# A two-block transformer step on one core: first rope angles on GpSimd, modulation columns by products with ones, lower parts of the first half on VectorE

## The chip, the cores and the metric

The kernel runs on one core of a Trainium2 chip, as one launch. The metric is the device time of the launch in microseconds (us), as the median of several runs.

## The reference, cut to what matters

Two blocks follow each other on one sequence of 1024 tokens of width 1024, all in float32. The first has two layers (differential attention with 8 heads, then latent attention with 8 heads), the second a layer of three mixers and a feed-forward part. Each layer begins in the same way:

```python
mod = silu(c) @ ada_w + ada_b                  # [1024] @ [1024, 3*1024]
shift, scale, gate = split(mod, 3)
h = rmsnorm(x, norm_g) * (1 + scale) + shift
proj = h @ w_in                                # q, k, v, z of all heads
q, k = rope(q, positions), rope(k, positions)  # cos and sin of positions * inv
...
x = x + gate * (o @ w_out)
```

So a layer's first projection needs `scale` and `shift`, each a sum over 1024 rows of a 1024 x 1024 block of `ada_w`, and the first scores need the cosines and sines of the positions.

## The kernel before, in words

Tokens lie along the free dimension: `h` is 8 chunks of 128 channels by two halves of 512 tokens. Every float32 operand of a large product is split into a rounded upper part ("hi") and a lower part ("lo", the rest), and a product of two operands is three products (`mm3`, line 192). The engines' instruction orders are made by a scheduler from the order in which the program is written, from priorities (`ahead`) and from costs that it assumes; each engine then works through its own list in order. All loads and stores are issued from SyncE (SP), also in order, with up to eight outstanding.

The start of layer 0 (`layer0`, line 899 on) is this:

- `load_x` loads x as 8 tiles of 128 tokens; `turn_x` squares and sums them on ScalarE, makes the reciprocal root mean (`rr`), and transposes the tiles on TensorE into `xt0` and `xt1`, one for each half of the tokens.
- `modulation_first` (lines 337 to 360) makes `scale0`, then `shift0`. Eight tiles of `ada_w` (128 rows of the sum each, 512 KB) are loaded into `h4` buffers. Tiles 0 to 3 are scaled by their element of silu(c) and added up on VectorE (lines 347 and 349) in `acc`; tiles 4 to 7 go through TensorE as products with a column of `cs` (line 352) into a row of 1024 sums in PSUM. `sum_cols` (lines 327 to 334) adds `acc` up over its 128 partitions: eight 128 x 128 transposes into two PSUM tiles and two VectorE reductions (line 334). The row in PSUM is copied by ScalarE (line 356) and turned into a column by eight one-row products with a one (line 359); line 360 adds the two.
- `rope_tables` (lines 250 to 279) loads the positions (line 261), makes the angles modulo 2 pi by eight instructions on VectorE (lines 265 to 273) and takes their absolute value, cosine and sine on ScalarE (lines 275 to 277), with a change of the activation table before and after (lines 276 and 279).
- `make_h` (lines 414 to 437) makes h = xt * acol * rr + shift in hi and lo. For half 0 the product is already there (`scaled`, line 915). Even chunks: ScalarE rounds hi (line 433) and VectorE makes lo (line 434). Odd chunks: ScalarE writes the sum (line 429) and rounds it (line 430), and GpSimd subtracts (line 169).
- `qk_rope` loads the first head's q and k weights (line 628), casts hi on ScalarE (line 632), makes lo on GpSimd (line 169), projects both halves (line 192: 96 products of 128 x 128 by 128 x 512 for the first head), turns them with the tables (lines 610 to 614) and moves the pieces into place by DMA (line 676, `move`). The scores (lines 681 and 682) read what was moved.

Later modulations (`modulation`, lines 297 to 325) have all eight tiles on VectorE (lines 316 and 318) and end in `sum_cols` as well: four in layer 0 during the heads (`late`), six for the second block during the heads of layer 1. Their tiles in layer 0 take `wr` buffers, of which there are two, shared with the weights.

## Time and profile before

| | |
|---|---|
| runs | 2959.03, 2968.55, 2955.31 us; median 2959.03 |
| profiled execution | 2964.13 us, its span 2962.4 us |
| TensorE products | 2646.8 us busy, 89% of the span |
| VectorE | 2118.1 us, 71% |
| ScalarE | 1437.1 us, 49% |
| GpSimd | 1291.4 us, 44% |
| mean granted TensorE clock | 0.951 |

Busy time of TensorE is modelled: products overlap, so 89% is not 89% of its peak. Times in the rows below are counted from the start of the span. A row of the timeline names the start, the duration, engine, line, operation and tiles, the number of instructions merged into it, and in brackets how long the engine had been idle and what ended the idling; DVE is VectorE, ACT ScalarE, POOL GpSimd, PE TensorE's products, PEld its weight loads, SPq the queue of SyncE.

### The profile page before, as it was taken

To read this page: it belongs to the slowest core of one execution; us is meant where nothing else is said; L and a number is where in the kernel's file an instruction comes from. 1 tells how busy PE (TensorE), PEld (TensorE's weight loads), DVE (VectorE), ACT (ScalarE), POOL (GpSimd) and SP (SyncE) were. 2 spreads that over 40 slices of the span, in tenths; PEclk is the share of its full clock that TensorE was granted. 3 is DMA by queue.
4 is the path that set the end of the run, shared out by engine and by line. 5 is a ranking of instruction groups with operands and counts; after the bars stand their busy time and mean duration, and the time that the engine had idled before them with its cause. 6 is when DMAs were issued, how large, how long until landed. Compare 5 with 4: busy or idle time off the path is not lost. (4 is left out here: it accounts for less than half of the span.)

```text
span 2962.4 us, 34674 instructions
## 1 busy us (share of the span) xinstructions
PE 2646.8 (89%) x12023; PEld 2136.0 (72%) x12023; DVE 2118.1 (71%) x2888; ACT 1437.1 (49%) x2609; POOL 1291.4 (44%) x775
## 2 busy tenths in 40 slices
PE   7889999899889989999987798887887999997897
PEld 4677777777777767787876587776776777775776
DVE  7687677766653377777677665578868888889874
ACT  5455455555543445454554454467544444444432
POOL 3233333333253352122234332244547887778760
PEclk8899999999999999999998899999998999998998
DMA  7534323233351263333333237424441222234564
GB/s 270 142 90 114 92 66 110 75 79 100 106 172 58 66 226 120 114 104 103 109 126 94 74 93 104 101 64 126 130 152 42 80 79 78 82 105 161 189 237 143
DMA packets 316850, 338.91 MB, mean 114 GB/s; under 512 B 37684, under 2 KB 240516, under 8 KB 316676
## 3 DMA queue, kind: packets, MB, share of 16 engines
q1 hardware_dynamic: 316676, 336.70, 38.6%
q8 instruction: 96, 1.57, 0.2%
q14 instruction: 78, 0.64, 0.1%
HBM read 231.17 MB, written 60.89 MB: 99 GB/s over the span
## 5 line engine op out<-in xcount | busy, mean ns | idle before, releaser
L192 PE MATMUL m<-h,wh 128*128 128x512 f32 x4744 | 1398.8, 404 | 62.3 <-ACT wh L183 16.2
L192 PEld LDWEIGHTS m<-h,wh 128*128 128x128 f32 x4744 | 910.4, 194 | 270.9 <-ACT wh L183 18.8
L192 PE MATMUL m<-h,wl 128*128 128x512 f32 x1472 | 589.8, 402 | 8.8 <-POOL wl L169 8.8
L169 POOL TENSOR_TENSOR wl<-wr,wh 128x1024 fp32r<-128x1024 f32 (+1 forms) x146 | 330.5, 2270 | 479.0 <-ACT wh L183 183.7
L761 ACT CAST pt<-m 128x256 fp32r<-128x256 f32 (+1 forms) x632 | 222.3, 370 | 289.9 <-PE m L757 158.3
L192 PEld LDWEIGHTS m<-h,wl 128*128 128x128 f32 x1472 | 286.9, 195 | 73.9 <-POOL wl L169 11.2
L169 DVE TENSOR_TENSOR pt<-m,pt 128x256 fp32r<-128x256 f32 (+2 forms) x652 | 256.3, 416 | 83.1 <-ACT pt L761 70.8
L741 ACT ACTIVATE e<-s,cf 128x1024 f32<-128x1024 f32 x192 | 214.9, 1121 | 155.1 <-DVE cf L738 139.1
L737 DVE TENSOR_REDUCE cf<-s 128x1 f32<-128x1024 f32 x192 | 232.4, 1217 | 75.8 <-PE s L682 40.5
L757 PE MATMUL m<-cr,e 128*128 128x128 f32 x1240 | 195.4, 282 | 32.9 <-DVE cf L738 14.3
L865 POOL TENSOR_SCALAR e<-e,cf 128x1024 f32<-128x1024 f32 x64 | 82.0, 1281 | 307.8 <-DVE cf L742 278.1
L192 PE MATMUL s<-h,wh 128*128 128x512 f32 x720 | 183.3, 400 | 36.4 <-DVE h L169 17.1
L681 PE MATMUL s<-kk,qq 128*128 128x512 f32 (+3 forms) x376 | 152.5, 411 | 52.6 <-ACT e L741 24.9
L757 PEld LDWEIGHTS m<-cr,e 128*128 128x128 f32 x1240 | 152.6, 145 | 61.5 <-issue 22.3
L1533 DVE SCALAR_TENSOR_TENSOR e<-z,cf,e 128x1023 f32<-128x1023 f32 (+1 forms) x88 | 175.8, 2008 | 24.8 <-ACT e L1531 24.6
L192 PE MATMUL m<-pt,v 128*128 128x512 f32 x768 | 188.7, 395 | 1.0 <-DVE pt L169 0.5
L192 PEld LDWEIGHTS s<-h,wh 128*128 128x128 f32 x720 | 136.9, 192 | 72.7 <-DVE h L169 18.6
L183 ACT CAST wh<-wr 128x1024 fp32r<-128x1024 f32 (+2 forms) x134 | 122.1, 915 | 110.6 <-PE m L192 47.2
L192 PEld LDWEIGHTS m<-pt,v 128*128 128x128 f32 x768 | 144.4, 190 | 32.3 <-DVE pt L169 1.6
L1105 POOL TENSOR_SCALAR e<-e,cf 128x1024 f32<-128x1024 f32 x64 | 73.7, 1154 | 186.6 <-DVE cf L742 182.7
L682 PE MATMUL s<-kk,qq 128*128 128x512 f32 (+3 forms) x376 | 144.4, 392 | 1.5 <-DMA qq<-pt 1.5
L169 DVE TENSOR_TENSOR wh<-wl,wh 128x512 fp32r<-128x512 f32 x90 | 121.7, 1370 | 19.4 <-ACT wh L443 19.2
(368 smaller groups left out, 4549.2 us busy)
## 6 DMA issues: line engine op xcount, KB each, us to landing
wr<-in_w_out_dram SPq DMA_DIRECT2D x48, 512.0 KB
tb<-in_w_ada_dram SPq DMA_DIRECT2D x48, 512.0 KB
wr<-in_w_up_dram SPq DMA_DIRECT2D x47, 512.0 KB
wr<-in_w_in_dram SPq DMA_DIRECT2D x45, 512.0 KB
qq<-ab SPq DMA_DIRECT2D x144, 128.0 KB
wr<-in_ada_w_dram SPq DMA_DIRECT2D x32, 512.0 KB
tf<-act SPq DMA_DIRECT2D x30, 512.0 KB
wr<-in_w_down_dram SPq DMA_DIRECT2D x30, 512.0 KB
```

Source lines behind the costliest of these rows:

```text
L169: (eng or self.nc.vector).tensor_sub(lo, src, hi.bitcast(F32))
L183: nc.scalar.copy(hi, raw)
L192: self.nc.tensor.matmul(out, l, r, start=start and n == 0, stop=stop and n == last)
L681: nc.tensor.matmul(ps, q(0, j), kk[:, ks], start=True, stop=False)
L682: nc.tensor.matmul(ps, q(1, j), kk[:, ks], start=False, stop=stop)
L737: nc.vector.reduce_max(nm, ps, axis=AX, negate=True)
L741: nc.scalar.activation(e, ps, AF.Exp, bias=nm, scale=scale, accum_out=sm)
L757: nc.tensor.transpose(ps[:, i], p[:, kt * 128:(kt + 1) * 128], self.ident)
L761: nc.scalar.copy(hi, ps[:, i:i + m])
L865: nc.gpsimd.tensor_scalar(e1, e1, r1, self.neglam, ALU.mult, ALU.mult)
L1105: nc.gpsimd.tensor_scalar(e, e, r, 1.0, ALU.mult, ALU.mult)
L1533: nc.vector.scalar_tensor_tensor(t[:, sh:], u[:, 0:S - sh], col(i), t[:, sh:], ALU.mult, ALU.add)
```

## The change

1. The first angles are made on GpSimd (`rope_angles(..., nc.gpsimd)`), and are written ahead of the loads of x; cosine and sine (`rope_sin`) stay where they were written. Multiplying by 1/(2 pi) and adding the magic number become one instruction, for both calls; on GpSimd each of the three scaled subtractions is two instructions.
2. `sum_cols` makes eight products of a 128 x 128 block of `acc` with a column of ones instead of eight transposes and two reductions, and its result is read in place by the addition of the bias. All later modulations use it.
3. In `modulation_first` VectorE takes five tiles and TensorE three; the sum on VectorE is added over its partitions by two products with the column of ones into the same PSUM row, and the row is turned by `sum_cols(row, 1)`.
4. In half 0 all eight chunks of h are made like the even ones: hi on ScalarE, lo on VectorE.
5. `load_x` and `turn_x` are called for each half; the tile that only takes the squares is a `tf` in place of a `z`.

```diff
     def rope_tables(self, nme):
+        self.rope_sin(self.rope_angles(nme, self.nc.vector))
+
+    def rope_angles(self, nme, eng):
...
-        nc.vector.tensor_copy(ang, pi)
-        nc.vector.tensor_scalar_mul(ang, ang, inv[:, 0:1])
+        eng.tensor_copy(ang, pi)
+        eng.tensor_scalar_mul(ang, ang, inv[:, 0:1])
         k = pi.bitcast(F32)
-        nc.vector.tensor_scalar_mul(k, ang, 1.0 / two_pi)
-        nc.vector.tensor_scalar_add(k, k, magic)
-        nc.vector.tensor_scalar_sub(k, k, magic)
+        eng.tensor_scalar(k, ang, 1.0 / two_pi, magic, ALU.mult, ALU.add)
+        eng.tensor_scalar_sub(k, k, magic)
         for cc in (c1, c2, c3):
-            nc.vector.scalar_tensor_tensor(ang, k, -cc, ang, ALU.mult, ALU.add)
-        nc.vector.tensor_scalar(ang, ang, lim, -lim, ALU.min, ALU.max)
+            if eng is nc.vector:
+                eng.scalar_tensor_tensor(ang, k, -cc, ang, ALU.mult, ALU.add)
+            else:
+                t = self.t("e", [128, S])
+                eng.tensor_scalar_mul(t, k, -cc)
+                eng.tensor_add(ang, ang, t)
+        eng.tensor_scalar(ang, ang, lim, -lim, ALU.min, ALU.max)
+        return ang, k
+
+    def rope_sin(self, angles):
...
-            self.sum_cols(acc, out)
-            nc.vector.tensor_add(out, out, bcol[:, g * 8:(g + 1) * 8])
+            nc.vector.tensor_add(out, self.sum_cols(acc), bcol[:, g * 8:(g + 1) * 8])
...
-    def sum_cols(self, acc, out):
-        for c0 in range(0, 8, 4):
-            ps = self.pm((128, 4, 128))
-            for j in range(4):
-                nc.tensor.transpose(ps[:, j], acc[:, (c0 + j) * 128:(c0 + j + 1) * 128], self.ident)
-            nc.vector.reduce_sum(out[:, c0:c0 + 4], ps, axis=AX)
+    def sum_cols(self, acc, n=128):
+        cols = self.pm((128, 8))
+        for j in range(8):
+            nc.tensor.matmul(
+                cols[:, j:j + 1], acc[0:n, j * 128:(j + 1) * 128], self.ones1[0:n], start=True, stop=True)
+        return cols
...
-            elif k < 4:
+                continue
+            if k < 5:
                 nc.vector.scalar_tensor_tensor(acc, wt, cs[:, k:k + 1], acc, ALU.mult, ALU.add)
-            else:
-                for i in range(0, 1024, 512):
-                    nc.tensor.matmul(ps[:, i:i + 512], cs[:, k:k + 1], wt[:, i:i + 512], start=k == 4, stop=k == 7)
-        self.sum_cols(acc, out)
-        nc.vector.tensor_add(out, out, bcol[:, g * 8:(g + 1) * 8])
+                continue
+            for i in range(0, 1024, 512):
+                nc.tensor.matmul(ps[:, i:i + 512], cs[:, k:k + 1], wt[:, i:i + 512], start=k == 5, stop=k == 7)
+                if k == 6:
+                    nc.tensor.matmul(ps[:, i:i + 512], self.ones1, acc[:, i:i + 512], start=False, stop=False)
         row = self.t("t2", [128, 1024])
         nc.scalar.copy(row[0:1], ps)
-        cols = self.pm((128, 8))
-        for j in range(8):
-            nc.tensor.matmul(cols[:, j:j + 1], row[0:1, j * 128:(j + 1) * 128], self.ones1[0:1], start=True, stop=True)
-        nc.vector.tensor_add(out, cols, out)
+        nc.vector.tensor_add(out, self.sum_cols(row, 1), bcol[:, g * 8:(g + 1) * 8])
...
-            if c % 2:
+            if c % 2 and scaled is None:
...
+        angles = self.rope_angles("positions", nc.gpsimd)
+        ss = self.small(8, "ss")
+        toks = [self.load_x(half) for half in range(2)]
+        (tiles0, xt0, rr0), (tiles1, xt1, rr1) = [self.turn_x(toks[half], half, ss) for half in range(2)]
...
-        self.rope_tables("positions")
+        self.rope_sin(angles)
```

The change also moves instructions in the lists. ScalarE, from the row copy of `scale0` (into `t_53`) to the first parts of h; `wh` are the cast weights of the first head, `tb` the tables. Before:

```order
L356 COPY t_53_460<-s_418 1x1024
L632 CAST wh_637<-wr_639 128x1024
L632 CAST wh_644<-wr_646 128x1024
L356 COPY t_71_528<-s_486 1x1024
L433 ACTIVATE h_77_559<-z_473,cf 128x512
...
L183 CAST wh_846<-wr_848 128x1024
L891 ACTIVATE cf<-cf 128x1 x2
L433 ACTIVATE h_95_619<-tf_617,cf 128x512
L276 ACT_TABLE_LOAD
L276 ACTIVATE tb_553<-e_540,cf 128x1024
L277 ACTIVATE tb_554<-e_543 128x1024
L279 ACT_TABLE_LOAD
```

In the changed kernel, from the row copy of `scale0` (into `t_57`):

```order
L369 COPY t_57_467<-s_437 1x1024
L288 ACTIVATE e_262<-e_265 128x1024
L638 CAST wh_615<-wr_617 128x1024
L289 ACT_TABLE_LOAD
L289 ACTIVATE tb_535<-e_262,cf 128x1024
L290 ACTIVATE tb_536<-e_265 128x1024
L292 ACT_TABLE_LOAD
L638 CAST wh_622<-wr_624 128x1024
L369 COPY t_73_523<-s_493 1x1024
L443 ACTIVATE h_77_541<-z_480,cf 128x512
L443 ACTIVATE h_78_544<-z_480,cf 128x512
```

The absolute value, the tables and both changes of table now stand ahead of the row copy of `shift0` (`t_73`; `t_71` before), with the first cast of the weights among them.

VectorE, from the end of half 1's products with `rr` to the first lower parts. Before:

```order
L424 SCALAR_TENSOR_TENSOR tf_607<-pt_350,cf,t_31_358 128x512 x2
L334 TENSOR_REDUCE cf<-m_515 128x4
L334 TENSOR_REDUCE cf<-m_521 128x4
L265 CAST e_543<-e_540 128x1024
L354 TENSOR_TENSOR cf<-cf 128x8
L266 TENSOR_SCALAR e_543<-e_543,cf 128x1024
L268 TENSOR_SCALAR e_540<-e_543 128x1024
L269 TENSOR_SCALAR e_540<-e_540 128x1024
L360 TENSOR_TENSOR cf<-m_530,cf 128x8
L270 TENSOR_SCALAR e_540<-e_540 128x1024
L272 SCALAR_TENSOR_TENSOR e_543<-e_540,e_543 128x1024
L434 SCALAR_TENSOR_TENSOR h_77_559<-z_473,cf,h_77_559 128x512
```

In the changed kernel:

```order
L434 SCALAR_TENSOR_TENSOR tf_585<-pt_369,cf,t_37_377 128x512 x2
L370 TENSOR_TENSOR cf<-m_525,cf 128x8
L444 SCALAR_TENSOR_TENSOR h_77_541<-z_480,cf,h_77_541 128x512
L444 SCALAR_TENSOR_TENSOR h_78_544<-z_480,cf,h_78_544 128x512
L444 SCALAR_TENSOR_TENSOR h_79_547<-z_481,cf,h_79_547 128x512
L444 SCALAR_TENSOR_TENSOR h_80_550<-z_481,cf,h_80_550 128x512
```

The addition that ends `shift0` has nothing of the angles or reductions around it.

VectorE, where the lower parts of the first head's second half of q and k (`ab`) stand beside the modulation tile of `gate0` (`t_137`). Before:

```order
L318 SCALAR_TENSOR_TENSOR t_137_888<-wr_1017,cf,t_137_888 128x1024
L169 TENSOR_TENSOR ab_784<-tf_786,ab_784 128x512
L169 TENSOR_TENSOR v_853<-m_881,v_852 128x512
L169 TENSOR_TENSOR ab_785<-tf_786,ab_785 128x512
L318 SCALAR_TENSOR_TENSOR t_137_888<-wr_1116,cf,t_137_888 128x1024
```

In the changed kernel:

```order
L169 TENSOR_TENSOR ab_762<-tf_764,ab_762 128x512
L169 TENSOR_TENSOR v_831<-m_859,v_830 128x512
L169 TENSOR_TENSOR ab_763<-tf_764,ab_763 128x512
L331 SCALAR_TENSOR_TENSOR t_137_866<-wr_995,cf,t_137_866 128x1024
L743 TENSOR_REDUCE cf<-s_914 128x1
```

A modulation tile that stood ahead of the lower parts stands behind them.

## Rows read from the trace of the kernel before

**Rows 1.** Busy time by stage: the stretch, its length, then busy us and instructions of each engine, the mean granted TensorE clock, the busy share of the DMA engines, GB/s.

```profile
20.00:30.00 10.00, 8.20 (x39) 3.62 (x36) 7.04 (x12) 1.78 (x5) 0.00 (x0) 1.00 1.03 410
...
53.00:86.00 33.00, 28.48 (x99) 20.34 (x99) 27.02 (x31) 23.51 (x36) 17.55 (x11) 0.82 0.27 79
...
99.00:115.00 16.00, 6.43 (x18) 4.45 (x19) 10.70 (x15) 4.53 (x9) 1.19 (x1) 0.61 0.82 219
...
120.00:800.00 680.00, 624.09 (x2876) 502.80 (x2875) 501.37 (x882) 372.34 (x714) 212.28 (x115) 0.96 0.33 91
...
1180.00:1480.00 300.00, 292.38 (x1507) 240.70 (x1506) 208.06 (x433) 153.74 (x360) 71.71 (x66) 1.00 0.36 106
```

**Rows 2.** Timeline of the first 60 us, TensorE: the eight one-row products that turn the row of `shift0` (16 records), and the first product with h.

```profile
47.41 1.94 PE L359 MATMUL m<-cf,t 1*128 1x1 f32 x16 [1.15 <-ACT t L356]
...
53.29 1.22 PE L192 MATMUL m<-h,wh 128*128 128x512 f32 x2 [3.94 <-ACT h L433]
```

**Rows 3.** Timeline of ScalarE: casts of the first weights, the row copy of `shift0`, the first part of h, and the tables.

```profile
40.90 1.04 ACT L632 CAST wh<-wr 128x1024 fp32r<-128x1024 f32 x1 [7.91 <-DMA wr<-in_w_in_dram]
...
42.31 1.04 ACT L632 CAST wh<-wr 128x1024 fp32r<-128x1024 f32 x1 [0.36 <-DMA wr<-in_w_in_dram]
...
46.36 1.00 ACT L356 COPY t<-s 1x1024 f32<-1x1024 f32 x1 [3.00 <-PE s L352]
...
52.51 0.72 ACT L433 ACTIVATE h<-z,cf 128x512 fp32r<-128x512 f32 x1 [5.15 <-DVE cf L360]
...
64.73 1.06 ACT L275 ACTIVATE e<-e 128x1024 f32<-128x1024 f32 x1
...
73.47 1.28 ACT L276 ACT_TABLE_LOAD   x1
...
74.77 1.15 ACT L276 ACTIVATE tb<-e,cf 128x1024 f32<-128x1024 f32 x1
...
75.83 1.04 ACT L277 ACTIVATE tb<-e 128x1024 f32<-128x1024 f32 x1
...
76.89 1.28 ACT L279 ACT_TABLE_LOAD   x1
```

**Rows 4.** Timeline of VectorE: half 1's products with `rr`, the start of the angles, the additions of `shift0`, lower parts of h, the last chunk's product, the first turn by the tables, a modulation tile.

```profile
41.27 4.06 DVE L424 SCALAR_TENSOR_TENSOR tf<-pt,cf,t 128x512 f32<-128x512 f32 x6
...
46.45 1.62 DVE L265 CAST e<-e 128x1024 f32<-128x1024 int32 x1
...
47.99 2.29 DVE L354 TENSOR_TENSOR cf<-cf 128x8 f32<-128x8 f32 x1
...
52.32 0.16 DVE L360 TENSOR_TENSOR cf<-m,cf 128x8 f32<-128x8 f32 x1
...
54.31 0.74 DVE L434 SCALAR_TENSOR_TENSOR h<-z,cf,h 128x512 fp32r<-128x512 f32 x1
...
64.63 1.65 DVE L434 SCALAR_TENSOR_TENSOR h<-tf,cf,h 128x512 fp32r<-128x512 f32 x1
...
71.95 0.74 DVE L424 SCALAR_TENSOR_TENSOR tf<-pt,cf,t 128x512 f32<-128x512 f32 x1
...
77.70 0.68 DVE L610 TENSOR_TENSOR tf<-m,tb 128x512 f32<-128x512 f32 x1
...
96.23 1.28 DVE L318 SCALAR_TENSOR_TENSOR t<-wr,cf,t 128x1024 f32<-128x1024 f32 x1 [8.38 <-DMA wr<-in_ada_w_dram]
```

**Rows 5.** Timeline of GpSimd: lower parts of the first weights, of h, a sum of 128 x 1024, a scaling of 128 x 1024.

```profile
42.03 8.23 POOL L169 TENSOR_TENSOR wl<-wr,wh 128x1024 fp32r<-128x1024 f32 x2 [39.88 <-ACT wh L632]
...
63.99 4.69 POOL L169 TENSOR_TENSOR h<-tf,h 128x512 fp32r<-128x512 f32 x3
...
80.86 2.38 POOL L614 TENSOR_TENSOR tf<-tf,tf 128x1024 f32<-128x1024 f32 x1
...
111.84 1.19 POOL L865 TENSOR_SCALAR e<-e,cf 128x1024 f32<-128x1024 f32 x1 [19.30 <-DVE cf L742]
```

**Rows 6.** Timeline of TensorE in the first head: 38 products from the first of these rows to the second; a wait; eight products from 81.97 to 85.30; the last of the projections; the first full scores.

```profile
68.05 0.39 PE L192 MATMUL m<-h,wl 128*128 128x512 f32 x1
...
76.73 0.39 PE L192 MATMUL m<-h,wh 128*128 128x512 f32 x1
...
77.85 0.50 PE L192 MATMUL m<-h,wh 128*128 128x512 f32 x1 [0.73 <-DVE h L434]
...
79.61 0.50 PE L192 MATMUL m<-h,wh 128*128 128x512 f32 x1 [1.03 <-ACT h L430]
...
81.97 0.97 PE L192 MATMUL m<-h,wh 128*128 128x512 f32 x2
...
85.30 0.47 PE L192 MATMUL m<-h,wl 128*128 128x512 f32 x1
...
103.71 0.77 PE L681 MATMUL s<-kk,qq 128*128 128x512 f32 x1 [0.95 <-DMA kk<-ab]
```

**Rows 7.** Groups of the first 150 us by line, engine, operation and shape: count, busy us and mean ns, idle us before.

```profile
L349 DVE SCALAR_TENSOR_TENSOR ab<-h,cf,ab 128x1024 f32<-128x1024 f32 x6 | 7.7, 1280 | 0.1
...
L268 DVE TENSOR_SCALAR e<-e 128x1024 f32<-128x1024 f32 x1 | 0.7, 693 | 0.0
```

**Rows 8.** Timeline at 1188 us, in layer 1: the transposes and reductions of one `sum_cols`.

```profile
1188.58 1.03 PE L333 MATMUL m<-cr,z 128*128 128x128 f32 x8
...
1189.22 0.69 DVE L334 TENSOR_REDUCE cf<-m 128x4 f32<-128x512 f32 x1
```

More of the change, by code (lines that the diff above doesn't have):

```diff
@@ L264, in rope_tables @@
         ang = self.t("e", [128, S])
-        nc.vector.tensor_copy(ang, pi)
-        nc.vector.tensor_scalar_mul(ang, ang, inv[:, 0:1])
+        eng.tensor_copy(ang, pi)
+        eng.tensor_scalar_mul(ang, ang, inv[:, 0:1])
         k = pi.bitcast(F32)
-        nc.vector.tensor_scalar_mul(k, ang, 1.0 / two_pi)
-        nc.vector.tensor_scalar_add(k, k, magic)
-        nc.vector.tensor_scalar_sub(k, k, magic)
+        eng.tensor_scalar(k, ang, 1.0 / two_pi, magic, ALU.mult, ALU.add)
+        eng.tensor_scalar_sub(k, k, magic)
         for cc in (c1, c2, c3):
-            nc.vector.scalar_tensor_tensor(ang, k, -cc, ang, ALU.mult, ALU.add)
-        nc.vector.tensor_scalar(ang, ang, lim, -lim, ALU.min, ALU.max)
+            if eng is nc.vector:
[7 more added lines that the diff above has]
+    def rope_sin(self, angles):
+        nc = self.nc
+        ang, k = angles
         cos, sin = self.t("tb", [128, S]), self.t("tb", [128, S])
@@ L557, in start_pairs, with load_x @@
             drain(g)
-    def load_x(self):
+    def load_x(self, half):
         nc, a = self.nc, self.a
         toks = []
-        for i in range(8):
-            tk = self.t(("kk", "qq")[i // 4], [128, 1024])
+        for i in range(4 * half, 4 * half + 4):
+            tk = self.t(("kk", "qq")[half], [128, 1024])
             nc.sync.dma_start(tk, a["x"][0, i * 128:(i + 1) * 128, :])
@@ L568, in load_x, with turn_x @@
         return toks
[L570 removed]
+    def turn_x(self, toks, half, ss):
         nc = self.nc
[L573 to L595 removed]
@@ new lines, in turn_x @@
+        junk = self.t("tf", [128, 1024])
+        tiles, xt = self.new_xt(("pt",) * 4)
+        hs = slice(4 * half, 4 * half + 4)
+        for i in range(4):
+            nc.scalar.activation(junk, toks[i], AF.Square, accum_out=ss[:, 4 * half + i:4 * half + i + 1])
+        self.rsqrt_mean(ss[:, hs], ss[:, hs], D)
+        t2 = self.t("t2", [128, 2, 512])
+        dg, rr = t2[:, 0].rearrange("p (a b) -> p a b", a=4), t2[:, 1]
+        ps = self.pS((128, 4, 128))
+        for i in range(4):
+            nc.vector.tensor_scalar_mul(dg[:, i], self.ident, ss[:, 4 * half + i:4 * half + i + 1])
+            nc.tensor.matmul(ps[:, i], self.ones_r.bitcast(F32), dg[:, i], start=True, stop=True)
@@ L598, in proj @@
+        nc.vector.tensor_copy(rr, ps.rearrange("p a b -> p (a b)"))
+        for c in range(8):
+            ps = self.pm((128, 4, 128))
+            for i in range(4):
+                nc.tensor.transpose(ps[:, i], toks[i][:, c * 128:(c + 1) * 128], self.ident)
+            (nc.vector.tensor_copy if c % 2 else nc.scalar.copy)(xt[c], ps.rearrange("p a b -> p (a b)"))
+        return tiles, xt, rr
     def proj(self, ws, hts, half, rows=128):
```

25 lines of the change are left out of this document (removed).

## The prediction, made before the changed kernel was run

> **What bounds the kernel now.** I read the stretches first, then the timeline of each engine over the first 105 us, then the groups by line and one later modulation.
>
> The stretches [rows 1] show two regimes. From 120 us on TensorE is busy 624 of 680 us, and in layer 1, from 1180 to 1480, 292 of 300 at a granted clock of 1.00: whatever adds TensorE work there adds time. The start is different. From 53 to 86 us TensorE makes the first head's 96 products and little else at a mean clock of 0.82, and from 99 to 115 it is busy 6.4 of 16 us. The 96 products need 0.228 us each at the full clock (38 products from 68.05 to 76.73, [rows 6]), so 21.9 us. They run from 53.29 [rows 2] to 85.77 [rows 6], 32.5 us. So 10.6 us go to gaps and to the low clock: eight products from 81.97 on start 0.416 us apart [rows 6], the level of 1.2 GHz, after gaps at 77.85, 79.61 and shortly behind.
>
> Who is waited for? h waits for `shift0`: its row is copied at 46.36 [rows 3], turned by 49.35 [rows 2], but added only at 52.32, because VectorE sits on the cast of the angles, on a tiny addition of 2.29 us, and on three more instructions of the angles [rows 4]. Then the lower parts come slowly: 1.65 us each beside GpSimd, 0.74 us without it [rows 4]. The late gaps wait for the last chunk of half 1, whose product with `rr` ran at 71.95 only [rows 4]. The first turn by the tables starts at 77.70 [rows 4], since the sine ended at 76.87 [rows 3]. And the lower parts of half 1's q and k stand behind a modulation tile that kept VectorE idle for 8.38 us until 96.23 [rows 4]. Full scores begin at 103.71, waiting for these moves [rows 6].
>
> **The start, part by part.** The positions go from behind the 16 modulation tiles to the head of SP's queue, past x and all tiles. Their 512 KB take 1.3 us at the 410 GB/s of rows 1, so x and the modulation tiles land about that much later. What stands behind both (the first head's weights) keeps its place in bytes, so its first cast stays at 40.90, where it waited for its data [rows 3]. The later tiles are covered by that, as the list below shows; without this cover they would cost 1.3 us.
>
> VectorE loses eight instructions of the angles, four reductions and two additions, and gains two tile additions of 1.28 us [rows 7] and four lower parts of 0.74 us [rows 4]. The two tile additions fall in the stretch in which it waits for tiles anyway. TensorE loses 16 transposes and four products on tiles, and gains four on `acc`: no more work before the row is copied.
>
> GpSimd gets 8 instructions with one tensor input and 3 with two. By the rows of its own, 1.19 and 2.38 us [rows 5], that is 9.5 + 7.1 = 16.6 us. That is without VectorE. Beside it two sums took 8.23 us [rows 5], while VectorE's six products ran undisturbed in 4.06 us [rows 4]: a factor 1.73, so 28.7 us at worst. The second instruction needs the `inv` column, issued behind four tiles of x; at 410 GB/s these and the positions take 6.4 us, and with some 5 us until the stream is going I estimate a start at 12 us. The end then lies between 29 and 41; I take 34, since VectorE is mostly on PSUM copies or waiting then.
>
> ScalarE decides when h starts. Its list now has the absolute value and the tables ahead of the row copy of `shift0`. From 40.90 on it does: cast 1.04, table change 1.28, 1.15, 1.04, table change 1.28, cast 1.04, row copy 1.00 [rows 3], in all 7.83 us, to 48.7. Turning the row takes 1.94 [rows 2], the addition 0.16 [rows 4] with nothing around it now. So the first h comes at 51.0, 1.5 us earlier than 52.51 [rows 3]: small, because 4.75 us of tables moved into this path.
>
> From there on half 0 needs 0.6 to 0.7 us a chunk on ScalarE and on VectorE, less than the 6 x 0.228 = 1.37 us a chunk of TensorE, so TensorE runs through. Half 1's last product with `rr` waits for the release of a buffer by the first lower part of half 1 on GpSimd, which no longer has four chunks of half 0 ahead of it, some 6 us at 1.56 us each [rows 5], but has a block of weights ahead, 2.4 to 4.1 us; VectorE no longer holds angles. I put it at about 65 instead of 71.95, ahead of TensorE's need. With 4 us at the low clock (10 products at 0.416) and 86 at 0.228 the projections end at 51.0 + 4.2 + 19.6 = 74.8 instead of 85.8: **11 us earlier**. The turn by the tables waits for nothing but the products (sine done at 45.4), so half 0's moves start about as much earlier, and the scores too. Bounds: 1.5 us if the gaps come back elsewhere in the same size, and 17 us if the modulation tile behind the lower parts also gives back most of its 8.4 us. I take 11, nearest to the count of products.
>
> **Later modulations.** Ten `sum_cols` change. Eight transposes take 1.03 us [rows 8]; eight products by a column are 16 records, which took 1.94 us with one-row weights [rows 2]. With 128 rows no row shows it; below it cannot be cheaper than 1.03, above I take twice the transposes, 2.06. I take 1.94: 0.9 us more each. The six in layer 1 fall into the stretch that is 97% busy: 5.4 us. The four in layer 0 meet 8% idle time; I count half, 1.8 us. VectorE is spared two reductions of 0.69 us each time [rows 8]; it is not the bound in either stretch, so I cost that at nothing; where it is waited for this is a gain, up to 1.4 us x 4 in layer 0. Joining two instructions of the angles saves 0.69 us of VectorE [rows 7] in the second call, hidden beside TensorE.
>
> Here a page of the Trainium skill reads otherwise: SBUF — State Buffer, section Who interferes with whom, has it that VectorE and GpSimd share a port pair as a lock that is held for a whole instruction, for VectorE instructions with two SBUF inputs or in its two-port modes. The pairs 0.74 and 1.65 us [rows 4] agree. By it the angles would not be free beside the modulation tiles, and the sum would be that of the fourth case, 2967, in place of 2955.
>
> **The sum.** 11 earlier, 5.4 + 1.8 later: 3.8 us gained, 2964.1 to about 2960.3 for the profiled execution. That execution lies 5.1 us above the median of 2959.03, so the median becomes **2955**. The lists of layer 0's heads are reordered by the scheduler as far as the fourth head; no row tells the sign of that. I allow 6 us either way, about a tenth of the 56 us that TensorE idles from 120 to 800 us [rows 1].
>
> **The rivals.** A measurement of this kernel tells about 0.5% from no change, 14.8 us: faster is below 2944.2, slower above 2973.8.
>
> *Forecast (0.50)*: the start is 11 us shorter, the columns cost 7; 2955, own range 2947 to 2962.
>
> *The start gains nothing (0.17)*: ScalarE's tables, now ahead of the row copy, eat the rest, or the gaps move to half 1's chunks. For it: the ScalarE list leaves only 1.5 us. Against it: the lower parts and the tables are surely earlier. 1.5 gained, 7 lost: 2959 + 5.5 = 2964.
>
> *More than counted (0.23)*: the modulation tile behind the lower parts gives its 8.4 us as well (17 in all), and the columns are hidden because TensorE's list shifts around waits, or VectorE's spared 1.4 us count. 17 less 3: 2945, down to 2939 with a good order. For it: the wait until 96.23 is the longest one of VectorE there. Against it: tiles from two shared buffers will be late somewhere else.
>
> *Slower (0.10)*: GpSimd's angles are late. The absolute value stands first in ScalarE's list, 1.06 us [rows 3], so from an end at 39.8 us on each us of GpSimd is a us of the start. At the factor 1.73 and with `inv` landing at 25 rather than 12 it ends at about 52: 1.06 and the casts, tables, copy, turn and addition follow (11.0 us), h starts at 63, 10.5 us later than before. The projections end at 63 + 23.8 = 86.8, 1 us later than before, and with the columns' 7 us the kernel takes 2967; with eight lower parts of half 0 also at 1.65 for 0.74 us, 2974. Against it: VectorE has gaps in this stretch. The page of the Trainium skill named above, SBUF — State Buffer, section Who interferes with whom, would expect this case wherever VectorE's queue keeps the port; rows 4 and 5 show that for a run of instructions without a gap alone.
>
> **How the numbers follow.** Faster: half of the third case and a twentieth of the first, 0.14 or so, with the noise of the order 0.17. Slower: half of the last and a few hundredths of the others' noise, 0.07. Within 0.5%: 0.76. Predicted 2955; the range from 2939 (third case's end) to 2969 (beyond the last case's 2967) leaves out about 2 in 10.
>
> **What would show it.** Right: first h (lower-part line, VectorE) at about 51 us; tables done on ScalarE by 47 us, ahead of the second weight cast; TensorE without gaps from about 55 to 75 us; the first full scores near 92 us; eight later products by ones at about 1.9 us each group, and the same idle share in layer 1. Wrong: an idle ScalarE in front of the absolute value that ends with GpSimd; a gap of TensorE before half 1's last chunk; the scores at 103 us again; or a lead at 105 us that is gone by 300 us, in which case the order of the heads and not the start sets the time.

## The result, and the profile of the changed kernel

The changed kernel takes 2999.31 us (2998.16 to 2999.81, 4 runs) against 2959.36 for the kernel before on the same chip: ratio 1.013, interval 1.0115 to 1.0146. The profiled execution has a span of 2997.7 us, 35.3 more than that of before. The forecast was 2955, between 2939 and 2969.

By stage, as in [rows 1]:

```profile
20.00:30.00 10.00, 5.61 (x37) 4.32 (x36) 9.46 (x14) 3.87 (x10) 9.78 (x4) 0.78 1.03 410
53.00:86.00 33.00, 26.71 (x111) 21.56 (x111) 27.70 (x38) 16.51 (x27) 13.79 (x8) 0.85 0.34 98
99.00:115.00 16.00, 8.55 (x34) 5.89 (x32) 10.31 (x14) 4.79 (x8) 1.20 (x1) 0.88 0.90 252
120.00:800.00 680.00, 620.05 (x2860) 500.70 (x2859) 476.16 (x838) 358.96 (x685) 210.61 (x112) 0.95 0.32 88
1180.00:1480.00 300.00, 294.69 (x1539) 244.78 (x1537) 198.37 (x418) 150.02 (x356) 72.52 (x68) 1.00 0.34 102
```

From 53 to 86 us TensorE has 26.7 us of products for 28.5 before, though they begin only at 59.3. From 120 to 800 us 2860 products stand where 2876 stood, at a clock of 0.95 for 0.96; layer 1 is denser than before.

The timeline of GpSimd: the angles, answering to the estimate made from [rows 5].

```profile
14.95 2.85 POOL L270 TENSOR_SCALAR e<-e,cf 128x1024 f32<-128x1024 f32 x1 [8.67 <-DMA cf<-in_inv_dram]
17.89 1.06 POOL L272 TENSOR_SCALAR e<-e 128x1024 f32<-128x1024 f32 x1
...
21.93 9.50 POOL L279 TENSOR_SCALAR e<-e 128x1024 f32<-128x1024 f32 x3
31.51 8.82 POOL L280 TENSOR_TENSOR e<-e,e 128x1024 f32<-128x1024 f32 x3
40.42 1.90 POOL L281 TENSOR_SCALAR e<-e 128x1024 f32<-128x1024 f32 x1
```

One scaling takes 1.06 us undisturbed and 3.17 in the group of three. The angles end at 42.3. VectorE beside them ([rows 4] before; 1.28 us a product of a tile in [rows 7]):

```profile
34.88 9.83 DVE L362 SCALAR_TENSOR_TENSOR ab<-h,cf,ab 128x1024 f32<-128x1024 f32 x4
44.63 0.16 DVE L370 TENSOR_TENSOR cf<-m,cf 128x8 f32<-128x8 f32 x1
44.82 2.12 DVE L375 SCALAR_TENSOR_TENSOR cf<-cf 128x8 f32<-128x8 f32 x1
46.98 2.74 DVE L923 SCALAR_TENSOR_TENSOR z<-pt,cf,t 128x512 f32<-128x512 f32 x4
49.63 4.82 DVE L923 SCALAR_TENSOR_TENSOR v<-pt,cf,t 128x512 f32<-128x512 f32 x4
54.38 4.05 DVE L434 SCALAR_TENSOR_TENSOR tf<-pt,cf,t 128x512 f32<-128x512 f32 x6
58.35 0.15 DVE L370 TENSOR_TENSOR cf<-m,cf 128x8 f32<-128x8 f32 x1
```

The four tile products take 2.46 us on average, and one by one they depend on what GpSimd does beside them. In this fence are a product beside a scaling of GpSimd (21.93 above), one beside a sum (L280), that sum, and the product behind the angles:

```profile
23.50 1.27 DVE L362 SCALAR_TENSOR_TENSOR ab<-h,cf,ab 128x1024 f32<-128x1024 f32 x1
...
34.88 3.25 DVE L362 SCALAR_TENSOR_TENSOR ab<-h,cf,ab 128x1024 f32<-128x1024 f32 x1
...
34.38 2.67 POOL L280 TENSOR_TENSOR e<-e,e 128x1024 f32<-128x1024 f32 x1
...
43.43 1.28 DVE L362 SCALAR_TENSOR_TENSOR ab<-h,cf,ab 128x1024 f32<-128x1024 f32 x1
```

An instruction on 8 columns took 2.12 us, beside a sum of GpSimd for the weights (44.45, 2.48 us). The addition of `shift0` (second L370) stands behind all of this. ScalarE, answering to [rows 3]:

```profile
42.35 1.06 ACT L288 ACTIVATE e<-e 128x1024 f32<-128x1024 f32 x1 [3.30 <-POOL e L281]
...
46.73 1.04 ACT L290 ACTIVATE tb<-e 128x1024 f32<-128x1024 f32 x1
...
50.04 1.00 ACT L369 COPY t<-s 1x1024 f32<-1x1024 f32 x1
58.54 2.56 ACT L443 ACTIVATE h<-z,cf 128x512 fp32r<-128x512 f32 x4 [7.50 <-DVE cf L370]
```

The first h comes at 58.54, 6 us later than in [rows 3], and ScalarE waits for VectorE's L370, not for the angles. TensorE, answering to [rows 2, 6, 8]; its first row is the turning of the row of `shift0`:

```profile
51.09 1.94 PE L344 MATMUL m<-cf,t 1*128 1x1 f32 x16 [1.87 <-ACT t L369]
...
59.31 2.07 PE L192 MATMUL m<-h,wh 128*128 128x512 f32 x4 [6.29 <-ACT h L443]
...
82.79 0.39 PE L192 MATMUL m<-h,wl 128*128 128x512 f32 x1
...
88.71 0.39 PE L192 MATMUL m<-h,wl 128*128 128x512 f32 x1
93.32 0.47 PE L687 MATMUL s<-kk,qq 128*128 128x512 f32 x1 [4.22 <-DMA kk<-ab]
...
104.11 0.47 PE L687 MATMUL s<-kk,qq 128*128 128x512 f32 x1 [1.15 <-DMA kk<-ab]
...
1206.31 1.84 PE L344 MATMUL m<-cf,z 128*128 128x1 f32 x16
1208.01 1.88 PE L192 MATMUL m<-pt,v 128*128 128x512 f32 x7
```

From 59.31 to 88.71 there is no gap, as forecast. The first head's 96 products end at 83.2, 23.9 us after their start for 23.8 in the forecast, and 2.6 us earlier than in [rows 6] although h came 6 us later. Then TensorE waits for moves, and the full scores come from 104 as before. What lies between are the first turn by the tables and the first move, here and then in the kernel before:

```profile
76.40 0.68 DVE L616 TENSOR_TENSOR tf<-m,tb 128x512 f32<-128x512 f32 x1
...
83.62 1.23 SPq L682 DMA_DIRECT2D kk<-ab  x2
```

```profile
83.91 1.23 SPq L676 DMA_DIRECT2D kk<-ab  x2
```

One group of column products holds TensorE for 1.70 us, from 1206.31 to the next start.

**Where the 35 us arise.** I matched ScalarE's instructions of two traces by line and tiles and took the difference of their starts, the lag, as a median over 25 us. Against the profile of before the changed kernel's lag is 0.2 us at 100, 19.1 at 1000, 17.6 at 1450, 29.3 at 1650 and about 35 from 2250 to the end. So: 19 in layer 0's heads, −1.5 in layer 1, 12 at its last head, 6 in block 2. Lags of all kernels are in the table behind the experiments; there, and in what follows, they are counted against a later execution of before (`e5`, the control).

### The profile page after: what moved, and what is told of

Read it like the earlier page. It is cut to its first block, busy times and chain, and to the rows that moved or that the text cites. A ratio compares the mean times of both kernels' runs of the same rounds, so it can differ in the third digit from the quotient of the medians.

```text
span 2997.7 us, 34751 instructions
## 1 busy us (share of the span) xinstructions
PE 2667.5 (89%) x12087; PEld 2158.1 (72%) x12087; DVE 2098.2 (70%) x2858; ACT 1436.5 (48%) x2605; POOL 1318.4 (44%) x782
## 5 line engine op out<-in xcount | busy, mean ns | idle before, releaser
L871 POOL TENSOR_SCALAR e<-e,cf 128x1024 f32<-128x1024 f32 x64 | 86.3, 1348 | 320.6 <-DVE cf L748 290.9
L1113 POOL TENSOR_SCALAR e<-e,cf 128x1024 f32<-128x1024 f32 x64 | 76.9, 1204 | 168.6 <-DVE cf L748 168.5
L687 PEld LDWEIGHTS s<-kk,qq 128*128 128x128 f32 x376 | 77.0, 206 | 85.4 <-ACT e L747 38.2
```

What stands on the lines that cost most here:

```text
L687: nc.tensor.matmul(ps, q(0, j), kk[:, ks], start=True, stop=False)
L871: nc.gpsimd.tensor_scalar(e1, e1, r1, self.neglam, ALU.mult, ALU.mult)
L1113: nc.gpsimd.tensor_scalar(e, e, r, 1.0, ALU.mult, ALU.mult)
```

## The experiments

Line numbers in a fence are those of its own kernel.

**Each part alone** (`e1` to `e4`).

```diff
# e1: the first angles on GpSimd, ahead of the loads; `rope_tables` split as in the change
+        angles = self.rope_angles("positions", nc.gpsimd)
# e2: sums by ones in `modulation`, `modulation_first` as before; `sum_ones` is the change's `sum_cols`
-            self.sum_cols(acc, out)
-            nc.vector.tensor_add(out, out, bcol[:, g * 8:(g + 1) * 8])
+            nc.vector.tensor_add(out, self.sum_ones(acc), bcol[:, g * 8:(g + 1) * 8])
# e3: `modulation_first` as in the change, the rest as before
# e4: lower parts of half 0
-            if c % 2:
+            if c % 2 and scaled is None:
```

> The kernel before with one part of the change alone: the first angles on GpSimd, written ahead of the loads of x (the two joined instructions of the angles are taken over too). Theory of the order (my first): the scheduler's lists of layer 0's heads, which every part of the change alters, set the time, and not the edited work; the time then moves where the lists differ. Here they differ mostly in the third and fourth of 25 parts of the program, and less than in any other part of the change: start late by up to 6 us (first h near 58 instead of 52.5), gone by 105 us, then between 6 us gained and 6 us lost in the heads until 700 us; total 2953 to 2967. Rival of the late angles: GpSimd's angles take the ports from VectorE and arrive late, the start is lost for good: first h near 58 and 6 us or more kept to the end, and most of the 35 us of the whole change shows here, 2975 or more.

> The kernel before with one part of the change alone: the ten later modulations sum over the partitions by eight products with the column of ones, and the first modulations are as before. Theory of the order: nothing up to 150 us, then a lag or lead between -10 and +20 us that arises by steps in layer 0's heads (150 to 700 us) where the lists differ, no growth from 1180 to 1460 us although six of the ten sums lie there, and a step of some 10 us between 1475 and 1625 us, where the lists of this kernel differ from before as those of the whole change do; total 2965 to 2985. Rival of the columns' cost: each of the ten groups costs TensorE 0.9 us or more, so the lag grows by 5 us evenly from 1180 to 1460 us and there is no step elsewhere; total 2965 to 2970. Rival of the late angles: no difference, 2959.

> The kernel before with one part of the change alone: in the first two modulations VectorE takes five tiles and TensorE three, and the sum goes over the partitions by two products with the column of ones. Theory of the order: the start is up to 3 us shorter, then 10 to 20 us are lost by steps in layer 0's heads (150 to 700 us), and a step of 5 to 8 us comes near 1850 us, where the lists of this kernel differ from before as those of the whole change do; total 2970 to 2985. Rivals of the late angles and of the columns' cost: the start gains 0 to 3 us and nothing else changes, 2956 to 2959.

> The kernel before with one part of the change alone: in half 0 all eight chunks have hi on ScalarE and lo on VectorE. Theory of the order: the first head's products end 2 to 6 us earlier, then a lag or lead of up to 20 us either way arises by steps in the first three heads (100 to 400 us) and once near 700 us, where the lists differ, and nothing after; total 2945 to 2980. Rivals of the late angles and of the columns' cost: the gain of the start is kept, 2953 to 2959.

Measured: 1.0037 (1.0018 to 1.0055), 1.0064 (1.0042 to 1.0086), 1.0037 (1.0020 to 1.0053), 1.0012 (0.9996 to 1.0028). `e1` has its first h at 58.4, is 5.7 us late at 100 us and 4.8 at 200, and keeps 7 at 1000, more than I expected of it: alone, the late angles cost the scores some 5 us. It did not make up most of the loss, as the rival wanted. `e2` loses nothing in layer 1 and 11 us at its last head, as the theory of the order said. `e3` leads by 5 us at 50 and is 10 late at 200. `e4` is 2 us ahead at 75 and 10 late at 200. The waits of TensorE that do it, `e3` and then `e4`:

```profile
186.65 0.79 PE L688 MATMUL s<-kk,qq 128*128 128x512 f32 x1 [5.09 <-ACT e L748]
...
219.32 1.19 PE L192 MATMUL m<-h,wh 128*128 128x512 f32 x2 [5.50 <-DVE cf L745]
```

```profile
186.37 0.80 PE L681 MATMUL s<-kk,qq 128*128 128x512 f32 x1 [5.09 <-ACT e L741]
...
219.56 1.19 PE L192 MATMUL m<-h,wh 128*128 128x512 f32 x2 [5.71 <-DVE cf L738]
```

Two edits with nothing in common make the same two waits; the longest of before between 170 and 230 us is 2.4. The changed kernel has them too (4.75 us at 184.52, 4.66 at 215.63). The four losses add up to 1.5%, near the whole; that this is no proof of a price for each, `e13` shows.

**A control, and the last head** (`e5` to `e7`).

```diff
# e6 against before: in `modulation`, for layer 1's sums alone
+            if acc_tag == "z":
+                nc.vector.tensor_add(out, self.sum_ones(acc), bcol[:, g * 8:(g + 1) * 8])
+            else:
...
# e7 against e6
-            self.mla_attention(7, *cur, vbox, kpe, zd, od, ots), 4, 4, ...
+            ahead(self.tc, self.mla_attention(7, *cur, vbox, kpe, zd, od, ots), 10), 4, 4, ...
```

> The kernel before, unchanged, profiled beside the next three on their chip, so that their lags are counted against an execution of the same chip; every theory expects a ratio of 1.00 within 0.3%. Of open interest: the four kernels with one part of the change each all lost 5 to 8 us between 1800 and 1880 us against the profile of before; if this execution loses them too, they belong to the execution and not to the change.

> The kernel before with products by the column of ones for the six later modulations of layer 1 alone; those of layer 0 keep their transposes. The lists are those of before up to 1100 us. Theory of the order: lag 0 until 1475 us (the five groups of column products that lie before it cost under 2 us together), a step of 10 to 13 us between 1475 and 1625 us, where the lists of the last head differ, none of it in the column products themselves; total 10 to 20 us over before. Rival of the columns' cost: 0.9 us for each group, so 4 to 5 us grown evenly by 1475 us, and at most 1 us after; total 5 to 6 over before. Rival of the late angles: 0.

> The kernel of the columns in layer 1 alone, with the same work and one difference: the attention of layer 1's last head has a scheduler priority of 10 (it had none), which reorders the lists between 1475 and 1625 us. Theory of the order: up to 1475 us as in that kernel; the step of 10 to 13 us between 1475 and 1625 us comes out otherwise, from 5 us gained to 25 lost, though every instruction is the same; that the attention waits less should make it smaller, I expect 0 to 8. Rivals of the columns' cost and of the late angles: no difference to that kernel beyond 2 us.

Measured: control 0.9982 (0.9963 to 1.0001); `e6` 1.0053 (1.0034 to 1.0071); `e7` 1.0026 (1.0004 to 1.0048). The control itself falls 16 us behind the first profile of before between 1725 and 1900 us, with the same lists: what the change seemed to lose in block 2 is of the size in which executions differ there. `e6` loses nothing up to 1475 us, then 11 by 1650. TensorE of `e6` there, and of the control:

```profile
1508.98 1.03 PE L769 MATMUL m<-cr,e 128*128 128x128 f32 x8
...
1515.99 0.39 PE L1115 MATMUL s<-h,h 128*128 128x512 f32 x1
1522.05 1.97 PE L769 MATMUL m<-cr,e 128*128 128x128 f32 x8 [5.67 <-POOL e L1117]
```

```profile
1482.15 0.39 PE L1103 MATMUL s<-h,h 128*128 128x512 f32 x1
...
1520.21 1.03 PE L757 MATMUL m<-cr,e 128*128 128x128 f32 x8
1526.54 5.60 PE L192 MATMUL m<-pt,v 128*128 128x512 f32 x24
```

In the control the last scores are issued by 1482, and 38 us of projections cover their softmax. In `e6` they stand behind those projections, and TensorE waits for the whole chain: reduction, exponential, reciprocal, scaling on GpSimd. Its mean clock from 1520 to 1540 is then 0.83 for 1.00. A second wait behind it, for cast weights, is 8.45 us (1606.69) for 4.32 in the control (1604.40). The changed kernel has the first wait, 5.68 us, in both of its profiles (1542.32 and 1540.54), and `e2` has it too. `e7`, the same instructions in another order, hasn't, and loses 7 in place of 11.

That leaves 7 us that this reordering did not give back. Every kernel with column products in layer 1 loses 3 to 14 us between 1475 and 1650 us, every other one less than 3, though the last of the sums ends ahead of this stretch. The kernel before with its last head at this priority was not run, so what of the 7 us belongs to that order isn't known.

**Before with other lists** (`e8`). `HP_A` is the scheduler's priority of the attention of layer 0's heads.

```diff
-HP_A = 10
+HP_A = 14
```

> The kernel before with no part of the change, but with a scheduler priority of 14 in place of 10 for the attention of layer 0's heads: the same instructions in other lists from about 130 to 800 us. Theory of the order: lag or lead by steps in that stretch and none outside of it but for 2 us, in all between 20 us lost and 10 gained, as large as what the whole change lost there (20). Rivals: both price instructions, not lists, and expect no difference beyond 4 us.

Measured: 1.0023 (1.0006 to 1.0040). All of its lag, 11 us at 1000, arises in layer 0, with no instruction changed.

**The change again, in other lists, and without the angles** (`e9`, `e10`, `e12`).

```diff
# e10 against the change (and the last head as in e7)
-HP_A = 10
+HP_A = 9
# e12 against the change
-        angles = self.rope_angles("positions", nc.gpsimd)
...
-        self.rope_sin(angles)
+        self.rope_tables("positions")
```

> The changed kernel once more, beside the next three on their chip, to see how much of its time belongs to an execution or a chip. Every theory expects 1.010 to 1.016 of the kernel before; the steps of its lag in layer 0's heads (about 20 us by 700 us) and in the last head of layer 1 (about 12 us) come back within 4 us, and what the first profile showed around 1830 us need not.

> The changed kernel with all of its parts and the same instructions, but a scheduler priority of 9 in place of 10 for the attention of layer 0's heads, and of 10 in place of none for that of layer 1's last head: other lists, in layer 0 nearer to those of the kernel before than the change's. Theory of the order: the lag of 20 us by 700 us comes out otherwise, I expect 5 to 15, and the 12 us of the last head at 4 to 8; total 10 to 25 us under the changed kernel. Rivals (late angles, columns' cost): the same time as the changed kernel within 4 us.

> The changed kernel with the first angles back on VectorE, where and when they were before; the other parts of the change stay. At the start: if GpSimd's instructions slowed VectorE's products of the modulation tiles (2.46 us each in the changed kernel, 1.28 before), they are back at 1.3 us and the first h comes 7 to 10 us earlier than the changed kernel's 58.5 us; if h had only waited for ScalarE behind the late angles, VectorE's products stay above 2 us. Total: theory of the order, 0 to 20 us under the changed kernel, by steps that do not follow the start; rival of the late angles, 6 us or more under it from the start on, constant to the end; rival of the columns' cost, within 3 us of it.

Measured: 1.0115 (1.0098 to 1.0133), 1.0057 (1.0035 to 1.0080), 1.0072 (1.0055 to 1.0090). `e9` repeats both steps: 16 us at 1000, 12 at the last head. `e10` is 20 us faster than `e9` (2991.76 for 3011.66) with every instruction of the change, the same late start (first h at 57.9) and the same two waits near 183 and 214 us; it gains in the later heads and at layer 1's last. `e12` tells why h was late. VectorE, the last row being the first turn by the tables:

```profile
31.64 3.93 DVE L362 SCALAR_TENSOR_TENSOR ab<-h,cf,ab 128x1024 f32<-128x1024 f32 x3 [0.92 <-DMA h<-in_ada_w_dram]
...
47.26 0.17 DVE L370 TENSOR_TENSOR cf<-m,cf 128x8 f32<-128x8 f32 x1 [1.41 <-PE m L344]
...
75.60 0.69 DVE L616 TENSOR_TENSOR tf<-m,tb 128x512 f32<-128x512 f32 x1 [2.17 <-ACT tb L289]
```

Without GpSimd the products are back at 1.31 us and the first h comes at 47.5, 11 us earlier. GpSimd had slowed VectorE; ScalarE's wait was a side show. Yet at 100 us its lag is about 1 us, at 150 also: the 11 us are gone by the scores. They go at the turn by the tables. With the angles back on VectorE the tables are late again, and the turn waits for them until 75.60, no earlier than in the changed kernel to speak of (76.40).

**The two other parts of the start** (`e11`): `e3` and `e4` together.

> The kernel before with two parts of the change, those that do not put work on GpSimd's or TensorE's list later on: the first two modulations with five tiles on VectorE and three on TensorE, and the lower parts of half 0 on VectorE; angles on VectorE and column sums as before. Without GpSimd's angles the start must show what these parts are worth there: first h at 47 to 49 us, 3 to 5 us earlier than before, the first head's products ended 6 to 9 us earlier, scores 3 to 8 us earlier. Theory of the order: this lead is kept or lost by steps of 5 to 12 us between 150 and 700 us as the lists fall; total between 8 us under and 15 over before. Rivals: the lead is kept, 4 to 8 us under before.

Measured: 1.0029 (1.0013 to 1.0044). First h at 48.15, as expected; the scores not earlier, against my expectation. TensorE, then ScalarE with the end of the tables and the second half's casts, then VectorE's first turn:

```profile
89.32 1.12 PE L711 MATMUL m<-cr,tf 128*128 128x128 f32 x4 [7.28 <-ACT tf L707]
...
103.02 0.47 PE L688 MATMUL s<-kk,qq 128*128 128x512 f32 x1 [1.78 <-DMA kk<-ab]
```

```profile
76.95 1.04 ACT L277 ACTIVATE tb<-e 128x1024 f32<-128x1024 f32 x1
...
95.06 0.62 ACT L624 CAST ab<-tf 128x512 fp32r<-128x512 f32 x1 [4.00 <-DMA kk<-ab]
96.96 0.62 ACT L624 CAST ab<-tf 128x512 fp32r<-128x512 f32 x1 [1.28 <-DMA kk<-ab]
```

```profile
77.98 0.69 DVE L617 TENSOR_TENSOR tf<-m,tb 128x512 f32<-128x512 f32 x1
```

TensorE ends early and idles 7.28 us. The first half's turn starts as the sine ends, at 77.98 (77.70 in [rows 4]), and its first move is issued at 83.66. The second half's q and k then wait for the two `ab` buffers, until the first half's moves have left them. So `e11` and `e12` have an early h and late tables, and the changed kernel has early tables and a late h; no run has both early.

**Parts with one or three steps written ahead** (`e13` to `e15`, `e17`). `LEAD0` is the number of steps of other work (projections, a modulation) written ahead of the attention of layer 0's first head. It acts on that head alone (`0 if h else LEAD0`), not on those from the second on, as the expectation of `e13` has it.

```diff
# e13 = e4, e15 = e11, e17 = before, each with
-LEAD0 = 2
+LEAD0 = 1
# e14 = e3 with
-LEAD0 = 2
+LEAD0 = 3
```

> The kernel with the lower parts of half 0 on VectorE alone, with one step in place of two of the next projections written ahead of each of layer 0's heads from the second on: the same instructions, lists of the first three heads nearer to those of before. Theory of the order: the 10 to 12 us that this part lost between 160 and 220 us shrink to under 6, total from 8 us under before to 6 over. Rivals (the parts' own work): as the part alone, 10 us lost by 220 us.

> The kernel with the changed first modulations alone, with three steps in place of two of the next projections written ahead of the heads: the same instructions, lists of the first three heads nearer to those of before. Theory of the order: the 11 to 12 us that this part lost between 160 and 220 us shrink to under 6, total from 8 us under before to 8 over. Rivals: as the part alone, 11 us lost to the end.

> The kernel with the changed first modulations and the lower parts of half 0 on VectorE, with one step in place of two written ahead of the heads. Theory of the order: other losses than the same parts with two steps (10 us by 220 us, 5 at the end); I expect a total from 8 us under before to 10 over, and if any of these kernels beats before it is one of this and the two just named. Rivals: the same as with two steps within 3 us.

> The kernel before with no part of the change, with one step in place of two written ahead of the heads: the control of the kernel that beat before. Theory of the order: the lists alone give what that kernel gained, 4 to 12 us under before, and the lower parts on VectorE give nothing or up to 3 us more. Rival (the lower parts' own work gains once the lists let it): the time of before within 4 us.

Measured: 0.9967 (0.9951 to 0.9983), 1.0056 (1.0041 to 1.0072), 0.9985 (0.9964 to 1.0006), 0.9995 (0.9979 to 1.0012). `e13` beats both kernels: 2970.94 us against 2981.69 for before. Between 110 and 208 us its TensorE has no wait over 0.9 us; the two waits of 5 us of `e4` are gone. From 7 us behind the control at 1000 the same instructions come to 7 ahead. `e14` was a miss: nearer lists, as I judged them, and a greater loss. `e15` came as expected. `e17`, the same step without the lower parts, gains nothing, against my expectation: this points to the edit's own work, which gains once its lists are good, but does not show it. The two ratios differ by 0.0028, their intervals touch, and they come from two chips.

**The change in two more sets of lists** (`e16`: `HP_A = 9`, `LEAD0 = 3`; `e18`: `LEAD0 = 1`; both with the last head as in `e7`).

> The changed kernel with all its parts, a priority of 9 for layer 0's heads, three steps written ahead of them, and a priority of 10 for layer 1's last head: a third set of lists of the same instructions, in layer 0 nearer to those of before than the change's and than the second set. Theory of the order: again 10 to 30 us under the changed kernel, total 1.000 to 1.008 of before. Rivals: the changed kernel's time within 4 us.

> The changed kernel with all its parts, one step in place of two written ahead of the heads and a priority of 10 for layer 1's last head: a fourth set of lists of the same instructions. Theory of the order: a time of its own between 0.998 and 1.014 of before, and by layer 0's part in the other kernels with one step I expect 5 to 25 us under the changed kernel. Rivals (late angles, columns' cost): the changed kernel's time within 4 us.

Measured: 1.0133 (1.0112 to 1.0154) and 1.0053 (1.0033 to 1.0072). `e16` was expected under the change and is not: as in `e14`, nearness to the old lists told nothing. TensorE of `e16`, the longest wait that the control hasn't:

```profile
118.94 0.80 PE L687 MATMUL s<-kk,qq 128*128 128x512 f32 x1 [9.18 <-ACT e L747]
```

The lags, in us, against the control (time in the control's span):

| kernel | 1000 | 1450 | 1650 | 2300 | ratio to before |
|---|---|---|---|---|---|
| before, first profile | 1.5 | −1.3 | −1.0 | −13.9 | |
| change, first profile | 20.6 | 16.3 | 28.3 | 21.0 | 1.0130 |
| change again (e9) | 16.0 | 14.6 | 26.7 | 30.5 | 1.0115 |
| change, other lists: e10 | 9.0 | 4.5 | 10.4 | 9.7 | 1.0057 |
| e16 | 32.5 | 29.0 | 32.0 | 39.7 | 1.0133 |
| e18 | 7.0 | 2.1 | 7.8 | 11.5 | 1.0053 |
| before, other lists: e8 | 11.2 | 11.5 | 12.8 | 8.5 | 1.0023 |
| e17 | 3.6 | 3.6 | 3.6 | −0.2 | 0.9995 |
| angles (e1) | 7.1 | 9.2 | 11.4 | 4.2 | 1.0037 |
| columns (e2) | 1.0 | 0.8 | 11.9 | 12.2 | 1.0064 |
| columns, layer 1 (e6) | −0.9 | −4.0 | 7.1 | 7.3 | 1.0053 |
| the same, last head ahead (e7) | −0.7 | −3.0 | 4.2 | 4.2 | 1.0026 |
| first modulations (e3) | 10.4 | 9.4 | 6.9 | 10.1 | 1.0037 |
| the same, three steps (e14) | 12.0 | 12.4 | 12.4 | 20.5 | 1.0056 |
| lower parts (e4) | 6.7 | 6.6 | 7.1 | 1.0 | 1.0012 |
| the same, one step (e13) | −6.7 | −10.0 | −9.4 | −2.7 | 0.9967 |
| both (e11) | 8.0 | 5.8 | 8.7 | 4.9 | 1.0029 |
| both, one step (e15) | −0.6 | −2.5 | −3.1 | 7.8 | 0.9985 |
| change without angles (e12) | 9.9 | 2.9 | 14.3 | 20.4 | 1.0072 |

The four sets of the change lie 7 to 32 us behind at 1000 us with the same instructions; two executions of one set differ by 5 there, and the control and the first profile of before by 1.5. How layer 0 loses its time is seen in TensorE's busy time between the same two points of the program, 110 and 800 us of the control; the changed kernel, then the control, columns as in [rows 1]:

```profile
110.60:821.70 711.10, 642.41 (x2931) 517.53 (x2932) 500.28 (x881) 377.33 (x720) 218.11 (x117) 0.94 0.33 90
```

```profile
110.00:800.00 690.00, 630.85 (x2899) 507.02 (x2900) 509.64 (x889) 375.76 (x720) 216.32 (x117) 0.96 0.34 92
```

Of the 21 us more, 9.5 are idle time of TensorE (68.7 us for 59.2) and 11.6 are busy time, at a lower clock and with four groups of column products in it. In the other sets of the change the idle time there is 61.7 us (`e10`), 74.5 (`e16`) and 61.6 (`e18`).

All four sets of the change are slower than all three of before: 1.0053 to 1.0133 against 0.9995 to 1.0023. So other lists gave back about half of the loss at best, and the change gained in none. Whether the rest is the price of its work or again of its lists, no run separates.

## Why the prediction was wrong, point by point

**The step that failed most** is the sentence "The lists of layer 0's heads are reordered by the scheduler as far as the fourth head; no row tells the sign of that. I allow 6 us either way." The change's lists lost 16 to 21 us there, and other lists of its instructions 7 to 32. That the range went wrong is worse than the sign: an allowance of a tenth of the idle time in [rows 1] had nothing to do with what a list can cost, since a bad one makes new idle time (59 us became 69, in `e16` 74.5) and a lower clock behind it. And layer 1's last head, where the lists differ too, had no term: 12 us. These two are about 31 of the 35 us between the profiles. That the order and not the work makes the loss is shown for the 20 us between `e9` and `e10`; for the rest it is argued.

**The start.** Forecast 11 us, found none at the scores. Four steps failed. The angles were put at 34 us and ended at 42.3: the second instruction started at 14.95 rather than 12, and from there on they took 27.4 us beside VectorE; the bound of 28.7 was the value to take. "The two tile additions fall in the stretch in which it waits for tiles anyway" was wrong: VectorE's products went from 1.28 us to 3.25 beside GpSimd's sums, 2.46 on average. I priced the contention on GpSimd's side and not on VectorE's. The Trainium skill (SBUF — State Buffer, section Who interferes with whom) has the port pair that the two engines share as an exclusive lock, for which a VectorE instruction with two inputs in SBUF contends. The 2.12 us of an 8-column instruction with two such inputs beside a sum of GpSimd, 0.17 in `e12` without one, agree. And "the addition 0.16 with nothing around it now" overlooked VectorE's own list: the row is turned by 53.0, but the addition of `shift0` stands behind six products of half 1 until 58.35. What follows was right as far as it goes: the 96 products take 23.9 us for 23.8, without a gap.

But "half 0's moves start about as much earlier, and the scores too" failed: the first move is issued at 83.62 for 83.91 before. The tables were ready at 47.8, but h was late, and when half 0's products are done VectorE still has products of half 1 and a modulation tile ahead of the first turn (76.40). In `e11` and `e12`, with h 10 us earlier than that, the tables hold the turn instead, until 77.98 and 75.60. Behind the moves the second half's casts wait for the `ab` buffers in the changed kernel (6.11 us, until 95.83) and in `e11`, and in all three the full scores come from 103 to 105. A late h is not free for that: `e1`, which has it without the lower parts on VectorE, lost some 5 us at the scores. What an early h and early tables give together was not run. The forecast's lower bound, 1.5 us if the gaps come back elsewhere, was nearest.

**The columns.** 0.9 us each was right: a group holds TensorE for 1.70 us, the transposes of [rows 8] for 0.79 (1188.58 to the next start at 1189.37). That six of them in the 97% busy stretch cost 5.4 us was wrong: from 1180 to 1475 us, where all six lie, the lag of `e6` goes from −3.5 to −4.5 and that of the changed kernel from 16.9 to 15.7. TensorE is 98% busy there instead of 97%: the work went into the gaps that were left.

**The rivals.** The fourth case's late h came, at 58.5 for its 63 and through VectorE more than ScalarE, but not its price: by 100 us the lag was 0.2. Two of the marks of being wrong came, the idle ScalarE ahead of the absolute value (3.30 us) and the scores at 103 again. The sign came from a case I had not made a rival. The last line of the prediction has it only for a lead that is gone by 300 us ("in which case the order of the heads and not the start sets the time"), and here there was no lead to lose; it deserved a chance and a range.

**Open.** Why one list loses 5 us at a place and another 10 is shown for single waits (the last head; 186 and 219 us; 119 us), not for all of layer 0. Whether the lower parts alone are worth 0.3% rests on `e13` against `e17`, on two chips. A kernel with the change's instructions and exactly the lists of before in the heads was not tried, so the half of the loss that stayed in every set of lists has no shown cause.

## What to carry to other kernels

Where a scheduler makes the lists, an edit is also a draw of new lists for everything behind it: price that draw by measured sets of the same instructions (here 0.3% for before, 0.8% for the change), and judge an edit by its best of several sets against the best of before. By that yardstick this change still loses, 1.0053 against 0.9995. Follow a gain at the start to the first point where two paths meet before it is booked, here the turn that needs projections, tables and a place in VectorE's list, and then buffers that a transfer must leave. Work moved to GpSimd beside two-input VectorE work is to be priced on both engines, at the durations of rows where they overlap.

## What the runs showed of the hardware that was not expected

Who pays where GpSimd and VectorE overlap depended on the instruction. Beside GpSimd's scalings (from 21.93 to 31.4) VectorE's tile products kept 1.27 to 1.45 us, and the scalings took 2.8 to 3.5 for 1.06. Beside GpSimd's sums (from 31.51 to 40.3) two products took 3.25 us each, and the sums 2.67 to 3.20 for 2.38.

GpSimd's scalings at 14.95 and 19.03 us took 2.85 and 2.81 us, 1.06 for one between them, while VectorE had almost only copies out of PSUM beside them, at their usual 0.64 to 0.69. The Trainium skill (SBUF — State Buffer, section Who interferes with whom) has VectorE instructions with at most one input from SBUF, outside the two-port modes, out of the contention; here GpSimd was slow beside them. Its cause was not tried: loads at 410 GB/s ran at the same time. And the kernel before has a median of 2959 us on one chip and of 2973 to 2982 on the others, more than most edits here are worth: only ratios within a chip can be compared.
